# A hybrid RG-LRU, HGRN2 and SSD trunk: running decay sums spread to all partitions by DMA from a scratch in memory, in place of selector matmuls, with the other changes of the same edit

## The chip, the cores and the metric

One core of one Trainium2 chip runs the whole kernel. The metric is the device time of one execution in microseconds (us); each run is timed and the median of the runs is given. A profiled execution of the same program gives the trace.

## The reference, cut to what matters

The input is one sequence of 2048 tokens of width 1024; there is one layer. It normalises, applies shift and scale from a conditioning vector, projects to 5648 columns, runs three recurrent branches, concatenates them, projects back, adds through a gate, and normalises again.

```python
mod = cond @ w_ada[l] + b_ada[l]
shift, scale, gate = jnp.split(mod, 3, axis=-1)
h = rmsnorm(x, norm_w[l]) * (1.0 + scale[:, None]) + shift[:, None]
u = h @ w_in[l]
...
ya = rg_lru(xa, ...) * jax.nn.silu(a_g)              # LRU branch
yb = rmsnorm(hgrn2_chunked(q_h, k_in, hg_i, log_f)) * jax.nn.silu(hg_g)
yc = ssd_chunked(xs_h, dt, A, Bm, Cm)                # SSD branch
y = jnp.concatenate([ya, yb, yc], axis=-1) @ w_out[l]
x = x + gate[:, None] * y
```

The change is in the SSD branch. Per chunk of 128 tokens and per head it needs the running sum `cum` of the decays, once down the partitions and once along the columns:

```python
cum = jnp.cumsum(ai, axis=1)
diff = cum[:, :, None] - cum[:, None, :]
L = jnp.where(causal, jnp.exp(jnp.where(causal, diff, 0.0)), 0.0)
cb = jnp.einsum('btgn,bsgn->btsg', ci, bi)
y = jnp.einsum('btsg,btsgj,bsgjp->btgjp', cb, L, xi)
y = y + jnp.einsum('btgn,bgjpn,btgj->btgjp', ci, state, jnp.exp(cum))
```

## The kernel before

Everything is fp32. Each operand of a projection is split into a high and a low half in a matmul format (`fp32r`), and three matmuls (`PASSES`) make one product. Time is cut into four blocks (`tb`) of 512 tokens, and the kernel works on two halves of two blocks each. Per half it goes through stages: HGRN2 (projections `ps_v`, `ps_f`, `ps_q`, `ps_g`), SSD (`ps_bc`, then eight blocks of 128 channels, each with `ps_x` and `ps_z`), LRU (four blocks, `ps_lx` and `ps_lg`). At the end the output projection (`po`) runs over all.

The order on TensorE (PE) is written by hand: `weave` takes the list of projection matmuls of the current step and puts the small matmuls of the branches (generators such as `ssd_a`, `ssd_b`, `lru`, `norm_gen`) between them, one step behind the projections that feed them. A number beside a branch (`l0` for the gate matmuls of `lru`) says how many places it takes, and so how far the next of its matmuls comes after the last. The orders on VectorE (DVE), ScalarE (ACT), GpSimd (POOL) and SyncE (SP, which issues most DMAs) come out of a scheduler. The first stage, in which weights and inputs still arrive, follows the table `PROG`: `Xn` loads the input of block n, `Dk` a piece of the conditioning weights, `Ak` and `Ck` the matmuls and columns of piece k, `w` and `W` fetch and split projection weights, `S` and `R` make the norm of a block, `Hnk` makes k-th tile `ht` (high by ACT, low by DVE) of block n, `Mnk` its nine projection matmuls, `K` constants, `U` warm-up matmuls.

Names that matter below. `ssd_cr` makes the running sums of all 16 heads as rows (`d_cr`). For each SSD block, time block and head, `ssd_a` broadcasts one row to all partitions with a matmul against a selector (`ps_bcr`, L741; 64 of them), DVE subtracts the column sum and takes the minimum with 0, per chunk (`s_m`, L745), ACT makes `exp` of the broadcast row (`s_ce`) and of the difference (`s_m`), DVE multiplies `s_m` by the masked scores, POOL multiplies `s_ce` by C. `ssd_b` makes the state from `ps_bx` and then `ps_y` from `s_m` and `s_ce`. Small tiles share one ring of 32 slots of 2 KB per partition.

Between the halves, the input of blocks 2 and 3 is loaded, normalised and made into `ht` for the second half during the last LRU blocks: `norm_stats` squares the input on ACT (`xr`), `norm_rows` spreads the inverse norm to all partitions (`ps_rb`), DVE scales (`xt`) and makes the low half (`ht`). LRU has the gate matmuls `ps_r` and `ps_i` (L826, L827), which wait for the convolution (`cacc`) on DVE. HGRN2 of the next half begins with `ps_v`, whose last 8 columns (`dtr`) DVE copies out (L379).

## Time and profile before

| what | value |
|---|---|
| three timed runs | 1720.01, 1720.40, 1721.47 us |
| median | 1720.4 us |
| profiled execution, its own time | 1718.6 us |
| its span, first to last instruction | 1716.8 us |
| PE matmul busy | 1669.7 us (97%) |
| PE weight loads busy | 1362.3 us (79%) |
| DVE, ACT, POOL busy | 1083.1 (63%), 669.7 (39%), 768.3 us (45%) |
| mean granted clock of TensorE | 0.991 |

Shares are of the span. PE's weight loads run beside its matmuls. A share is a mean over stages that differ, so it does not tell by itself which engine is waited for in a stage.

### The profile page before, as it was taken

To read this page: it belongs to the slowest core of one execution; us is meant where nothing else is said; L and a number is where in the kernel's file an instruction comes from. 1 tells how busy PE (TensorE), PEld (TensorE's weight loads), DVE (VectorE), ACT (ScalarE), POOL (GpSimd) and SP (SyncE) were. 2 spreads that over 40 slices of the span, in tenths; PEclk is the share of its full clock that TensorE was granted. 3 is DMA by queue.
4 is the path that set the end of the run, shared out by engine and by line. 5 is a ranking of instruction groups with operands and counts; after the bars stand their busy time and mean duration, and the time that the engine had idled before them with its cause. 6 is when DMAs were issued, how large, how long until landed. Compare 5 with 4: busy or idle time off the path is not lost.

```text
span 1716.8 us, 29450 instructions
## 1 busy us (share of the span) xinstructions
PE 1669.7 (97%) x11520; PEld 1362.3 (79%) x11520; DVE 1083.1 (63%) x2042; ACT 669.7 (39%) x1346; POOL 768.3 (45%) x630
## 2 busy tenths in 40 slices
...
DMA packets 168492, 133.72 MB, mean 78 GB/s; under 512 B 13600, under 2 KB 136992, under 8 KB 168352
## 3 DMA queue, kind: packets, MB, share of 16 engines
...
## 4 chain that ended last, share of the span: by engine, by line
PE 84%; ACT 4%; DVE 4%; DMA 3%; issue 3%; POOL 2%; SPq 0%; ACTq 0%; POOLq 0%; DVEq 0%
PE po L1126 19%; PE ps_z L338 10%; PE ps_x L338 10%; PE ps_v L344 5%; PE ps_f L338 5%; PE ps_g L338 5%; PE ps_bc L338 5%; PE ps_q L338 4%; PE ps_lx L338 3%; PE ps_lg L338 2%; PE ps_y L789 2%; PE ps_bx L765 2%; PE ps_y L794 1%; PE ps_sA L562 1%; DVE xt L72 1%
## 5 line engine op out<-in xcount | busy, mean ns | idle before, releaser
L1126 PE MATMUL po<-wo,yy 128*128 128x512 f32 x1512 | 353.7, 396 | 2.6 <-POOL yy L69 1.6
L1126 PEld LDWEIGHTS po<-wo,yy 128*128 128x128 f32 x1512 | 284.0, 188 | 71.8 <-POOL yy L69 2.4
L69 POOL TENSOR_TENSOR w<-raw,w 128x512 fp32r<-128x512 f32 x156 | 223.5, 1451 | 209.3 <-ACT w L141 191.0
L72 DVE SCALAR_TENSOR_TENSOR cacc<-craw,col,cacc 128x512 f32<-128x512 f32 x192 | 205.9, 1079 | 47.7 <-ACT cacc L66 38.3
L338 PE MATMUL ps_x<-ht,w 128*128 128x512 f32 x768 | 192.4, 398 | 0.0
L338 PE MATMUL ps_z<-ht,w 128*128 128x512 f32 x768 | 189.8, 399 | 0.0
L338 PEld LDWEIGHTS ps_z<-ht,w 128*128 128x128 f32 x768 | 142.0, 189 | 33.4 <-issue 2.1
L338 PEld LDWEIGHTS ps_x<-ht,w 128*128 128x128 f32 x768 | 142.9, 189 | 29.9
L72 DVE SCALAR_TENSOR_TENSOR o<-po,rstd,o 128x512 f32<-128x512 f32 x64 | 47.3, 750 | 121.6 <-PE po L1126 103.1
L69 POOL TENSOR_TENSOR yy<-yr,yy 128x512 fp32r<-128x512 f32 x61 | 79.7, 1325 | 80.5 <-ACT yy L66 68.8
L69 POOL TENSOR_TENSOR hg_k<-hg_k,hg_t 128x256 f32<-128x256 f32 x80 | 59.1, 754 | 121.8 <-PE ps_sA L562 62.2
L338 PE MATMUL ps_f<-ht,w 128*128 128x512 f32 x384 | 99.6, 406 | 7.5 <-DVE ht L72 4.9
L344 PE MATMUL ps_v<-vw,ht 128*128 128x264 f32 x768 | 99.6, 290 | 4.8 <-DVE dtr L379 4.8
L141 ACT ACTIVATE w<-raw 128x512 fp32r<-128x512 f32 x156 | 90.3, 625 | 34.9 <-issue 22.3
L338 PE MATMUL ps_bc<-ht,w 128*128 128x512 f32 x384 | 101.2, 405 | 0.0
L344 PEld LDWEIGHTS ps_v<-vw,ht 128*128 128x128 f32 x768 | 96.3, 192 | 6.2 <-DVE dtr L379 5.0
L69 POOL TENSOR_TENSOR s_ce<-s_ce,cacc 128x512 f32<-128x512 f32 x64 | 100.1, 1581 | 1.1 <-ACT s_ce L66 0.8
L338 PE MATMUL ps_lx<-ht,w 128*128 128x512 f32 x384 | 99.5, 412 | 0.0
L338 PE MATMUL ps_q<-ht,w 128*128 128x512 f32 x384 | 99.2, 404 | 0.0
L338 PE MATMUL ps_lg<-ht,w 128*128 128x512 f32 x384 | 93.2, 398 | 0.0
L338 PE MATMUL ps_g<-ht,w 128*128 128x512 f32 x336 | 91.9, 408 | 0.0
L338 PEld LDWEIGHTS ps_f<-ht,w 128*128 128x128 f32 x384 | 70.9, 191 | 26.3 <-DVE ht L72 5.6
...
## 6 DMA issues: line engine op xcount, KB each, us to landing
raw<-in_w_in SPq DMA_DIRECT2D x176, 256.0 KB, 3.1
yr<-yscr SPq DMA_DIRECT2D x64, 256.0 KB, 3.2
xr<-in_x SPq DMA_DIRECT2D x48, 256.0 KB, 3.4
xt<-in_x_t SPq DMA_DIRECT2D x32, 256.0 KB, 5.3
wta<-in_w_mod SPq DMA_DIRECT2D x32, 256.0 KB, 5.3
yscr<-cacc ACTq DMA_DIRECT2D x32, 256.0 KB, 2.3
rawo<-in_w_out SPq DMA_DIRECT2D x32, 256.0 KB, 4.0
out<-o POOLq DMA_DIRECT2D x30, 256.0 KB, 3.6
```

The source lines that it names most:

```text
L69: e.tensor_tensor(o, a, b, op=op)
L72: V.scalar_tensor_tensor(o, a, s, b, op0=op0, op1=op1)
L141: after(V.tensor_copy(hi, raw) if eng is V else S.activation(hi, raw, AF.Copy), dep)
L338: d_ = PE.matmul(ps, b.hl[wl][:, k, :], ht[:, hl, :], start=(k == 0 and n == 0), stop=(k == KT - 1 and n == 2))
L344: d_ = PE.matmul(ps[:, 0:264], ht[:, hl, c * P:(c + 1) * P], b.vw[k // 4][wl][:, k % 4, :], start=(k == 0 and n == 0), stop=(k == KT - 1 a ...
L562: PE.matmul(out(n, c, r), Ks[n][:, o:o + 32], mv[n][..., o + sh:o + sh + 32], start=True, stop=True)
L765: PE.matmul(pkv[:, c].rearrange("p h n -> p (h n)"), bt[:, c], xw[:, c].rearrange("p h n -> p (h n)"), start=True, stop=True)
L789: PE.matmul(py[64 * hh:64 * hh + 64, c], xdt[:, c, hh], Ms[hh][:, c], start=True, stop=sv[tb][c] is None)
L794: PE.matmul(py[64 * hh:64 * hh + 64, c], sv[tb][c][:, 64 * hh:64 * hh + 64], Cs[hh][:, c * P:(c + 1) * P], start=False, stop=True)
L1126: PE.matmul(pss[t, n], yys[u, t][yl][:, k4, :], wts[4 * fam + k4][wl][n], start=(k4 == 0 and i == 0), stop=(k4 == 3 and i == 2))
```

## The change

The selector `sel`, its input `onehot_in` and the matmuls `ps_bcr` go. ACT copies the 16 rows of running sums to SBUF, a DMA writes them to a scratch in memory (`crd`), and for each SSD block, time block and head a DMA reads one row back with all 128 partitions as its destination (`s_cb`, 64 transfers of 256 KB). They are issued after the block's projections have been written down, ahead of the step in which `ssd_a` uses them. DVE's 256 subtractions become 256 `Relu` activations of 128x128 on ACT (scale -1, the column sum as bias), and the `exp` behind them takes scale -1.

Beside that: `PROG` is rewritten (weights of the second kind fetched later, `D2`, `X1` and the norm of block 0 earlier, constants `K` later), the softplus constants are made at the start (`early`) instead of in `consts`; `dtr` is copied by ACT instead of DVE; `norm_stats` of the second half moves from LRU steps 0 and 1 to SSD group 1, steps 1 and 2, and its inverse root to `norm_gen`; the second pair of gate matmuls of LRU step 2 in the first half comes later (`l0 = 2`), into another PSUM bank; two warm-up matmuls fewer; `split` on DVE makes the high half on ACT; `aneg` is made later.

```diff
-        cr = tmp("d_cr", (P, TB), F32R)
-        prf = pr.rearrange("p c n -> p (c n)")
-        V.tensor_copy(cr, prf)
-        for o in (32, 96):
-            tt(V, cr[o:o + 8], prf[o:o + 8], cr[o:o + 8], SUB)
-        return cr
+        cr = tmp("d_cr")
+        act(cr[0:16], pr.rearrange("p c n -> p (c n)")[0:16], AF.Copy)
+        nc.sync.dma_start(crd[tb], cr[0:16])
+
+    def ssd_cb(i, tb):
+        r = []
+        for hh in range(2):
+            cb = tmp("s_cb")
+            h_ = 2 * i + hh
+            nc.sync.dma_start(cb, crd[tb][h_:h_ + 1, :].to_broadcast([P, TB]))
+            r.append(cb)
+        return r
...
         for hh in range(2):
-            pb = bank(ps_sc, "sc", "ps_bcr", (P, 4, P))
-            PE.matmul(pb.rearrange("p c n -> p (c n)"), sel[:, g, 2 * j + hh:2 * j + hh + 1].to_broadcast([P, P]), cr,
-                      start=True, stop=True)
-            m = tmp("s_m", (P, 4, P))
+            m = cbs[tb][hh].rearrange("p (c n) -> p c n", n=P)
+            ce = tmp("s_ce")
+            act(ce, cbs[tb][hh], AF.Exp)
             for c in range(4):
-                V.tensor_scalar(m[:, c], pb[:, c], cum[:, c, h0 + hh:h0 + hh + 1], 0.0, op0=SUB, op1=MIN)
-            ce = tmp("s_ce")
-            act(ce, pb.rearrange("p c n -> p (c n)"), AF.Exp)
-            act(m, m, AF.Exp)
+                act(m[:, c], m[:, c], AF.Relu, scale=-1.0, bias=cum[:, c, h0 + hh:h0 + hh + 1])
+            act(m, m, AF.Exp, scale=-1.0)
             tt(V, m, m, gm, MUL)
             tt(G, ce, ce, C2, MUL)
...
-        V.tensor_copy(dtr[:, c, 8 * p:8 * p + 8], ps[:, 256:264])
+        act(dtr[:, c, 8 * p:8 * p + 8], ps[:, 256:264], AF.Copy)
...
+                if half == 0 and g == 1 and j in (1, 2):
+                    xst[j - 1] = norm_stats(1 + j)
...
                 sr = {}
-                pend = [(ssd_a(g, j, tb, xz[0, tb], bcg, dts[tb][0], sr), 2) for tb in tbs]
+                cbs = {tb: ssd_cb(4 * g + j, tb) for tb in tbs}
+                pend = [(ssd_a(g, j, tb, xz[0, tb], bcg, dts[tb][0], cbs, sr), 2) for tb in tbs]
...
-            if i < 2 and half == 0:
-                xst[i] = norm_stats(2 + i)
...
-            l0 = 5 if i == 3 and half == 1 else L0
+            l0 = 5 if i == 3 and half == 1 else 2 if i == 2 and half == 0 else L0
...
-PROG = ("X0 D0 w0 D1 w1 D2 S0 U8 A0 U1 C0 U2 R0 W0 D3 A1 U1 C1 H00 D4 W1 A2 M00 C2 H01 D5 A3 M01 C3 H02 D6 A4 M02 C4 "
-        "H03 D7 A5 M03 C5 H04 X1 A6 M04 C6 H05 S1 A7 M05 C7 H06 K M06 H07 R1 B M07 H10 H11 M10 H12 M11 H13 M12 H14 M13 "
-        "H15 M14 H16 M15 H17 M16 M17")
+PROG = ("X0 D0 w0 D1 D2 S0 U8 A0 Q0 U1 C0 D3 R0 W0 A1 U1 C1 H00 D4 A2 M00 C2 H01 w1 W1 D5 A3 M01 C3 H02 D6 A4 M02 C4 H03 X1 "
+        "A5 M03 C5 H04 D7 A6 M04 C6 H05 S1 M05 H06 Q1 A7 R1 M06 C7 H10 H07 B K M10 H11 M11 H12 M07 H13 M12 H14 M13 "
+        "H15 M14 H16 M15 H17 E M16 M17")
```

The rows of the orders follow at three places; an `x` and a number at the end of a row count equal rows in a run.

First place: PE in the SSD stage of the first half, the matmuls from the end of one block's `ps_z` to its `ps_bx`. Before:

```order
L338 MATMUL ps_z<-ht,w 128x512 x15
L733 MATMUL ps_xtr<-ident,cacc 128x128 x4
L741 MATMUL ps_bcr<-d_cr,sel 128x512
L338 MATMUL ps_x<-ht,w 128x512 x9
L741 MATMUL ps_bcr<-d_cr,sel 128x512
L338 MATMUL ps_x<-ht,w 128x512 x6
L733 MATMUL ps_xtr<-ident,cacc 128x128 x4
L741 MATMUL ps_bcr<-d_cr,sel 128x512
L338 MATMUL ps_x<-ht,w 128x512 x6
L741 MATMUL ps_bcr<-d_cr,sel 128x512
L338 MATMUL ps_x<-ht,w 128x512 x12
```

In the change:

```order
L339 MATMUL ps_z<-ht,w 128x512 x15
L739 MATMUL ps_xtr<-ident,cacc 128x128 x4
L339 MATMUL ps_x<-ht,w 128x512 x15
L739 MATMUL ps_xtr<-ident,cacc 128x128 x4
L339 MATMUL ps_x<-ht,w 128x512 x18
L768 MATMUL ps_bx<-s_xw,s_btok 128x128 x4
L339 MATMUL ps_x<-ht,w 128x512 x15
```

The four `ps_bcr` of a block are gone; the projections on either side of each stand together now.

Second place, between the halves: PE around the two pairs of gate matmuls (`ps_r`, `ps_i`) of LRU step 2 (steps count from 0). Before:

```order
L826 MATMUL ps_r<-cacc,wab 128x512
L827 MATMUL ps_i<-cacc,wab 128x512
L338 MATMUL ps_lx<-ht,w 128x512 x3
L826 MATMUL ps_r<-cacc,wab 128x512
L827 MATMUL ps_i<-cacc,wab 128x512
L338 MATMUL ps_lx<-ht,w 128x512 x21
L338 MATMUL ps_lg<-ht,w 128x512 x24
L338 MATMUL ps_lx<-ht,w 128x512 x24
L338 MATMUL ps_lg<-ht,w 128x512 x24
```

In the change:

```order
L829 MATMUL ps_r<-cacc,wab 128x512
L830 MATMUL ps_i<-cacc,wab 128x512
L339 MATMUL ps_lx<-ht,w 128x512 x21
L829 MATMUL ps_r<-cacc,wab 128x512
L830 MATMUL ps_i<-cacc,wab 128x512
L339 MATMUL ps_lx<-ht,w 128x512 x3
L339 MATMUL ps_lg<-ht,w 128x512 x24
L339 MATMUL ps_lx<-ht,w 128x512 x24
L339 MATMUL ps_lg<-ht,w 128x512 x24
```

Of the two gate pairs, the second stands behind 21 `ps_lx` now, where 3 stood before. At the same place, a little later, DVE's rows around the scaling of the input of block 3 (`xt`). Before:

```order
L72 SCALAR_TENSOR_TENSOR cacc<-craw,col,cacc 128x512
L69 TENSOR_TENSOR l_gs<-l_gs,ps_lg 128x512
L72 SCALAR_TENSOR_TENSOR cacc<-craw,col,cacc 128x512 x2
L72 SCALAR_TENSOR_TENSOR xt<-xt,gsc,rb 128x512 x8
L72 SCALAR_TENSOR_TENSOR ht<-xt,gsc,ht 128x512
L379 COPY dtr<-ps_v 128x8
L72 SCALAR_TENSOR_TENSOR ht<-xt,gsc,ht 128x512 x4
L379 COPY dtr<-ps_v 128x8
```

In the change:

```order
L72 SCALAR_TENSOR_TENSOR cacc<-craw,col,cacc 128x512
L69 TENSOR_TENSOR l_gs<-l_gs,ps_lg 128x512
L72 SCALAR_TENSOR_TENSOR cacc<-craw,col,cacc 128x512 x2
L285 RECIPROCAL xst<-xst 128x4
L72 SCALAR_TENSOR_TENSOR xt<-xt,gsc,rb 128x512 x8
L72 SCALAR_TENSOR_TENSOR ht<-xt,gsc,ht 128x512 x8
```

The copies of `dtr` have left DVE, and the reciprocal of the norm (`xst`), for which the second `ps_rb` waits, has come in behind the convolutions (`cacc`).

Third place, the start: DVE from the first scaling of block 1's input (`xt`) on. Before:

```order
L72 SCALAR_TENSOR_TENSOR xt<-xt,gsc,rb 128x512
L69 TENSOR_TENSOR sp_p<-sp_p,sp_w 128x4
L72 SCALAR_TENSOR_TENSOR xt<-xt,gsc,rb 128x512 x7
L136 TENSOR_SCALAR sp_p<-sp_p 128x4
L72 SCALAR_TENSOR_TENSOR hg_q<-hg_q,omlb,ps_q 128x512
L533 TENSOR_SCALAR hg_f<-hg_f,omlb 128x512
L72 SCALAR_TENSOR_TENSOR ht<-xt,gsc,ht 128x512
L72 SCALAR_TENSOR_TENSOR hg_g<-hg_g,col,ps_g 128x512
L72 SCALAR_TENSOR_TENSOR ht<-xt,gsc,ht 128x512 x2
```

In the change:

```order
L314 RECIPROCAL xsc<-xsc 128x4
L470 COPY maskd<-mf 128x32
L471 CAST masks<-mf 128x160
L72 SCALAR_TENSOR_TENSOR xt<-xt,gsc,rb 128x512 x7
L72 SCALAR_TENSOR_TENSOR ht<-xt,gsc,ht 128x512
L72 SCALAR_TENSOR_TENSOR gsc<-psm,col 128x1
L69 TENSOR_TENSOR gsc<-psm,col 128x1
L1048 TENSOR_SCALAR aneg<-aneg 128x16
L69 TENSOR_TENSOR gsc<-gsc,col 128x1
L72 SCALAR_TENSOR_TENSOR xt<-xt,gsc,rb 128x512 x2
L72 SCALAR_TENSOR_TENSOR ht<-xt,gsc,ht 128x512 x8
```

In both orders seven `xt` stand ahead of the first low half `ht` that follows; in the change the softplus rows (`sp_p`) are gone from between them, and the sign change of `aneg` (L1048) has come in.

## Rows read from the trace of the kernel before

**Rows 1.** The page's first part: busy time, share of span and instructions by engine.

```profile
PE 1669.7 (97%) x11520; PEld 1362.3 (79%) x11520; DVE 1083.1 (63%) x2042; ACT 669.7 (39%) x1346; POOL 768.3 (45%) x630
```

**Rows 2.** Windows: length; busy PE, PEld, DVE, ACT, POOL; clock; DMA share; GB/s.

```profile
0.00:50.00 50.00, 44.50 (x260) 26.22 (x261) 28.09 (x75) 23.96 (x45) 7.17 (x13) 1.00 0.93 311
50.00:100.00 50.00, 40.73 (x394) 34.67 (x393) 35.92 (x85) 19.29 (x39) 15.75 (x13) 0.90 0.31 82
350.00:450.00 100.00, 100.00 (x611) 83.30 (x610) 83.12 (x164) 44.72 (x93) 62.62 (x45) 1.00 0.19 53
650.00:750.00 100.00, 87.28 (x436) 71.65 (x435) 66.62 (x89) 57.08 (x105) 47.05 (x36) 0.91 0.28 77
```

**Rows 3.** Waits of PE: what it waited for, total us, times, longest us.

```profile
PE ps_f L338 <- DVE ht L72: 4.9, 2, 4.6
...
PE ps_f L338 <- ACT ht L330: 2.4, 2, 1.5
...
PE ps_rb L320 <- DVE sp_w L129: 2.0, 1, 2.0
```

**Rows 4.** Timeline of PE, one SSD block: start us, duration us, engine, line, operation.

```profile
400.35 0.48 PE L741 MATMUL ps_bcr<-d_cr,sel 128*128 128x512 f32 x1
400.67 2.26 PE L338 MATMUL ps_x<-ht,w 128*128 128x512 f32 x9
402.77 0.39 PE L741 MATMUL ps_bcr<-d_cr,sel 128*128 128x512 f32 x1
403.00 1.55 PE L338 MATMUL ps_x<-ht,w 128*128 128x512 f32 x6
```

**Rows 5.** The same timeline, later: the first ps_y of that block.

```profile
423.22 0.66 PE L789 MATMUL ps_y<-s_m,s_xdt 128*64 128x128 f32 x8
```

**Rows 6.** Timeline of DVE: the last product of scores and decay of that block.

```profile
410.58 1.12 DVE L69 TENSOR_TENSOR s_m<-s_m,s_gm 128x512 f32<-128x512 f32 x1 [0.34 <-ACT s_m L66]
```

**Rows 7.** Groups of ACT by form: xcount, then busy us and mean ns of one.

```profile
L66 ACT ACTIVATE hg_v<-ps_v 128x128 f32<-128x128 f32 x64 | 14.2, 273 | 70.2 <-PE ps_v L344 62.9 <-POOL l_gs L69 7.3
```

**Rows 8.** DMA issues: count, KB each, median us from issue to landing.

```profile
br<-in_rows SPq DMA_DIRECT2D x2, 256.0 KB, 4.2
```

**Rows 9.** Timeline of PE at the start; brackets: idle before, releaser.

```profile
54.78 1.63 PE L338 MATMUL ps_f<-ht,w 128*128 128x512 f32 x3
...
64.61 1.22 PE L338 MATMUL ps_f<-ht,w 128*128 128x512 f32 x2 [4.64 <-DVE ht L72]
65.63 1.48 PE L338 MATMUL ps_q<-ht,w 128*128 128x512 f32 x3
66.91 1.48 PE L338 MATMUL ps_g<-ht,wt 128*128 128x512 f32 x3
```

**Rows 10.** Timeline of DVE at the start: the scaling of block 1's input.

```profile
56.53 4.72 DVE L72 SCALAR_TENSOR_TENSOR xt<-xt,gsc,rb 128x512 f32<-128x512 f32 x7
```

**Rows 11.** Timeline of PE between the halves.

```profile
670.06 2.07 PE L826 MATMUL ps_r<-cacc,wab 128*128 128x512 f32 x2 [7.74 <-DVE cacc L72]
...
672.85 6.88 PE L338 MATMUL ps_lx<-ht,w 128*128 128x512 f32 x21
679.57 5.77 PE L338 MATMUL ps_lg<-ht,w 128*128 128x512 f32 x24
...
698.79 1.05 PE L320 MATMUL ps_rb<-ident,xst 128*128 128x128 f32 x8
699.60 8.27 PE L344 MATMUL ps_v<-vw,ht 128*128 128x264 f32 x66
712.65 5.07 PE L344 MATMUL ps_v<-vw,ht 128*128 128x264 f32 x24 [4.78 <-DVE dtr L379]
```

**Rows 12.** Timeline of DVE between the halves.

```profile
660.93 7.41 DVE L72 SCALAR_TENSOR_TENSOR xt<-xt,gsc,rb 128x512 f32<-128x512 f32 x8
...
699.72 2.68 DVE L72 SCALAR_TENSOR_TENSOR cacc<-craw,col,cacc 128x512 f32<-128x512 f32 x2
702.33 9.53 DVE L72 SCALAR_TENSOR_TENSOR xt<-xt,gsc,rb 128x512 f32<-128x512 f32 x8
```

More of the change, by code (lines that the diff above doesn't have):

```diff
@@ L88, in trunk @@
     rowp = cpool.tile([P, 32], F32, name="rowp")
-    ohf = cpool.tile([P, 2, 8], F32, name="ohf")
     wab = cpool.tile([P, 2, 4, P], F32, name="wab")
@@ L102, in trunk @@
     rstd = cpool.tile([P, 3, 16], F32, name="rstd")
+    crd = [dpool.tile([16, TB], F32, name=f"crd{i}") for i in range(NTB)]
     yscr = [dpool.tile([4, P, 16, P], F32, name=f"yscr{i}") for i in range(NTB)]
@@ L321, in norm_rows @@
         rb = tmp("rb")
-        d_ = S.activation(rb, ps, AF.Copy)
-        return rb, d_.ins.name
+        act(rb, ps, AF.Copy)
+        return rb
     def h_pre(xs, rb, k):
```

93 lines of the change are left out of this document (48 added, 45 removed).

## The prediction

> **What bounds the kernel now.** I read the page's busy times first. PE's matmuls take 97% of the span and no other engine more than 63% [rows 1], so time is won in two ways only: PE gets less to do, or it stands still less. The windows tell where each counts. In the SSD stage (350 to 450 us) PE is busy 100.00 of 100 us at the full clock, with DVE at 83.12 and ACT at 44.72 [rows 2]: there every matmul taken away is time taken away, as long as nothing else comes late. In two other windows PE has holes: 50 to 100 us (40.73 of 50 busy, granted clock 0.90) and 650 to 750 us (87.28 of 100, clock 0.91) [rows 2]. The list of PE's waits and the timelines name them. At the start PE waits for `ht`, by DVE 4.9 and by ACT 2.4 us, and 2.0 us for a softplus row ahead of the row of norms [rows 3]; 4.64 of the 4.9 is one wait [rows 9]. Between the halves it waits 7.74 us for `cacc` and 4.78 us for `dtr`, both on DVE [rows 11], and both times DVE is scaling eight `xt` tiles, 7.41 and 9.53 us [rows 12]. After such a hole PE runs at half clock (1.2 GHz) for a while: three matmuls start 1.28 us apart (65.63 to 66.91) [rows 9], where in the SSD stage nine take 2.10 us, that is 0.70 for three [rows 4].
>
> So there are three places, and the change touches each.
>
> **SSD stage.** 64 `ps_bcr` go, four in each of 16 blocks. What one costs is read from start to start in the timeline, since durations overlap: 0.32 us (400.35 to 400.67) and 0.23 us (402.77 to 403.00) [rows 4]; the other two of the block are alike (0.31 and 0.23). The mean of 0.27 gives 64 x 0.27 = **17.3 us**. Bounds: all at 0.23 give 14.7 us, and at the row's full 0.48 at most 31; as PE is without a hole there I take 17.3 and hold 14.7 to 20 for likely. The Trainium skill (TensorE: Matmul & The Clock Gate, Back-to-back issue gap) has a sustained spacing of some 131 ns for 512 columns; by that the 64 would be worth an estimated 8.4 us and the sum below 8.9 us less. The row speaks against it for this kernel: nine such matmuls in 2.10 us are 0.233 each [rows 4].
>
> The gain holds if the new way is hidden. DVE loses 256 subtractions, which only relieves it. ACT gets 16 `Relu` of 128x128 in each block. The nearest row is a copy of that shape, 64 in 14.2 us busy, 0.22 us each, 273 ns if alone [rows 7]: 3.6 to 4.4 us more on some 13.2 us of ACT in the 29.5 us of a block (44.72% [rows 2]), so 17 to 18, or 60%. The Trainium skill speaks against this move (ScalarE: Activation LUTs, Rules for kernel authors: simple arithmetic such as relu belongs on VectorE), and gives some 93 ns more for each operand that is a column. With that an estimated 5 us would be added to a block, which still leaves ACT idle for a third of it, so here the rule costs nothing by itself. The broadcasts, 64 of 256 KB, go to SP's queue among the weights. The nearest row is `br`, a row spread over all partitions in the same way: 4.2 us from issue to landing [rows 8]. They are issued about a step before they are needed. A block's last product of scores and decay ends at 411.70 (410.58 + 1.12) [rows 6], and the first `ps_y` that needs it starts at 423.22 [rows 5]: 11.5 us of slack before, and of the same order after. I cost them at nothing; if that cover is gone, the price is in the third rival.
>
> **Start.** The holes for `ht`, rb and ACT sum to 4.9 + 2.4 + 2.0 = 9.3 us [rows 3]. From 54.78 to the end of the three at 66.91 [rows 9] 18 matmuls run at half clock, at 1.28 - 0.70 = 0.58 us for each three: 3.5 us. So 12.8 us can be had. `D2` and the norm go ahead of the second weights `w1`, three transfers of 256 KB; at the 311 GB/s of the first 50 us [rows 2] these are 2.5 us, and I take 2 for the earlier start of the first projections. What stays: in the new order seven `xt` still stand ahead of the first low half of block 1, as the rows of the third place show, and they take 4.72 us [rows 10]. Input `X1` is moved past `D7`, four transfers of 256 KB, 3.4 us at that rate, so a part of the 4.72 is hidden: I keep 3.5 us of it. For `aneg`, which now stands among these rows and waits for the late load of `rowp`, I choose 1.2 us, with no row to size it, and 2.3 us for half clock after the hole: 7 in all. The start gains 12.8 + 2 - 7 = **7.8 us**, between 4 and 15.
>
> **Between the halves.** The second pair of gate matmuls stands 18 `ps_lx` later, 18 x 0.233 = 4.2 us more for DVE, and only five of the eight `xt` stand ahead of its `cacc`. The squares `xr` have left ACT at this place, so that the LRU chain runs ahead. I take the wait of 7.74 us as gone, and with it the half clock behind it: 21 `ps_lx` in 6.72 us (672.85 to 679.57) where 24 `ps_lg` take 5.77 at full clock, that is 5.05 for 21, so 1.7; the four gate matmuls take 2.79 (670.06 to 672.85), about twice their time, so 1.4 [rows 11]. With ACT copying `dtr`, the 4.78 us go too, and the half clock after them: 24 `ps_v` in 5.07 us against 66 in 8.27, or 3.0 for 24, so 2.1 us [rows 11]. Together 7.74 + 3.1 + 4.78 + 2.1 = 17.7 us.
>
> What is late next: the second `ps_rb` now needs the reciprocal of the norm, and that stands on DVE behind the two `cacc` that ended at 702.40 (699.72 + 2.68) [rows 12], while `ps_rb` itself started at 698.79 [rows 11]. With the same distance PE waits 3.6 us plus the reciprocal, 3.8 in all, and I add 2 us of half clock as after the hole for `dtr`. Left: 17.7 - 5.8 = **11.9 us**, between 6 (a second hole of this kind) and 17.7 (none).
>
> **Sum.** 17.3 + 7.8 + 11.9 = 37.0 us. The trace's own time is 1718.6 us (span 1716.8 and 1.8 around it), so 1681.6; the median of the runs shown lies 1.8 above the traced execution, so about **1683 us**.
>
> **The rivals.**
> *No hole is left.* Both `ps_rb` and the tiles of block 1 come in time: 17.3 + 14.8 + 17.7 = 49.8, which gives about 1671 us. For it: every wait named above has its cause moved. Against: the orders show `xt` ahead of `ht` and the reciprocal behind `cacc`.
> *The holes only move.* Projections are there in time but wait for another tile of the same engines: SSD at its lower bound 14.7, start 4, middle 2. That gives 20.7, about 1700 us. For it: DVE has the same eight `xt` and `ht` to do between the halves, busy 66.62 of 100 us [rows 2] with holes in PE all the same.
> *The broadcast chain becomes the bound of SSD.* ACT works in order. If a broadcast lands late, because SP's queue stands behind a slot of the ring that is not free, the `Relu` and `exp` that wait for it hold up ACT's evacuation of `ps_x`, and PE waits in each of 16 blocks. From 37.0 / 16 = 2.3 us a block on, the kernel is slower than before; at 3 us a block it is 1683 + 48 = 1731 us. For it: four slots of 32 are held a step longer, and ACT has more in its queue. Against: 11.5 us of slack [rows 5, 6] and ACT at 60%.
>
> **How the numbers follow.** Forecast 0.58, no hole 0.15, holes move 0.17, chain 0.10. A change under 0.2% (3.4 us) can't be told from none here. Of the chain's chance I give 0.06 to slower, 0.02 to the same and 0.02 to faster; the others are faster but for 0.01 of the moved holes: faster 0.91, same 0.03, slower 0.06. The range goes from 1668, just past the case without holes (SSD at 20 instead of 17.3), to 1703, just past the case of moved holes: it leaves out most of the chain and the tails of the others, some 0.15 to 0.2.
>
> **What would show it.** In the SSD windows PE stays at 100 of 100 us with no wait of `ps_y` or `ps_x` for `s_cb`, a block starts every 28.4 to 28.5 us in place of 29.54, and ACT's share is near 60. At the start `ps_f` still waits some 3 to 4 us for DVE's `ht`, and the first `ps_sA` comes some 7 us earlier. Between the halves no wait for `dtr` is left, the wait for `cacc` at `ps_r` is under 1 us, and `ps_rb` waits 3 to 5 us for the reciprocal. The prediction is wrong if `ps_y` waits for DVE or ACT in many blocks, or if a wait of over 5 us stands where none is named here.

## The result and the profile after

| | median | lowest to highest | runs |
|---|---|---|---|
| before | 1720.93 us | 1720.01 to 1721.68 | 4 |
| changed | 1700.57 us | 1699.24 to 1702.20 | 4 |

The changed kernel takes 0.9887 of the time before (95% interval 0.9875 to 0.9899): 20.4 us less. The forecast was 1683 us, 37 us less, in a range of 1668 to 1703. So the sign and the range held, the range by 2 us at its slow end, and little more than half (55%) of the gain that was added up came. The profiled execution has a span of 1697.5 us, 19.3 less than before.

The page's head, to be held against [rows 1]: busy time of each engine.

```profile
span 1697.5 us, 29336 instructions
...
PE 1653.0 (97%) x11452; PEld 1349.2 (79%) x11452; DVE 971.5 (57%) x1726; ACT 748.6 (44%) x1640; POOL 757.3 (45%) x630
```

PE has 16.7 us less to do, DVE 112 us less and ACT 79 us more. The windows, to be held against [rows 2]:

```profile
0.00:50.00 50.00, 41.13 (x230) 23.91 (x230) 28.78 (x94) 24.61 (x46) 6.11 (x12) 0.96 0.98 318
50.00:100.00 50.00, 41.62 (x338) 34.84 (x339) 33.13 (x57) 19.83 (x42) 15.70 (x12) 0.87 0.29 75
350.00:450.00 100.00, 100.00 (x611) 83.33 (x610) 65.31 (x120) 64.25 (x158) 61.90 (x47) 1.00 0.31 89
650.00:750.00 100.00, 94.49 (x479) 78.83 (x479) 60.91 (x82) 58.27 (x109) 46.53 (x37) 0.97 0.32 90
```

The SSD window is full as before, with DVE at 65.31 and ACT at 64.25. Between the halves PE is busy 94.49 us where it was 87.28. But the start, 0 to 100 us, is worse: 82.75 us busy in place of 85.23, at a lower clock. The list of PE's waits says why, to be held against [rows 3]:

```profile
PE ps_rb L320 <- DVE xst L285: 7.3, 2, 5.5
PE ps_f L339 <- DVE ht L72: 5.4, 1, 5.4
PE ps_ss L311 <- DVE xsq L305: 3.9, 1, 3.9
PE psm L450 <- ACT macc L66: 2.9, 1, 2.9
...
PE ps_z L339 <- ACT halo L66: 0.8, 1, 0.8
...
PE ps_y L792 <- DVE s_cb L69: 0.8, 1, 0.8
PE ps_xtr L739 <- DVE sst L72: 0.6, 1, 0.6
```

The waits for `cacc` (7.74 us) and `dtr` (4.78 us) [rows 11] are gone, and at the start those for ACT's `ht` (2.4) and the softplus row (2.0) [rows 3]. New are 7.3 us at `ps_rb`, 3.9 us for the squares of block 1 (`xsq`), 2.9 us for a column sum (`macc`), and 2.2 us in the SSD stage (`ps_z`, `ps_y`, `ps_xtr`). The wait for `ht` is still there.

Where the time went, by the starts of the same matmuls in the two traces (us; each line is a stretch up to the matmul named):

| up to | before | changed | this stretch | forecast |
|---|---|---|---|---|
| first `ps_sA` (start stage done) | 82.95 | 85.89 | +2.9 | -7.8 |
| first `ps_x` (HGRN2, half 1) | 314.54 | 317.56 | +0.1 | 0 |
| first `ps_r` (SSD, half 1) | 605.61 | 602.96 | -5.7 | -8.7 |
| `ps_f` of half 2 (between the halves) | 717.56 | 707.21 | -7.7 | -11.9 |
| first `po` (half 2, with its SSD) | 1344.3 | 1326.2 | -7.8 | -8.6 |
| end of span | 1716.8 | 1697.5 | -1.2 | 0 |

The lines that answer to [rows 4]: PE in one SSD block, with the start of `ps_bx` in this block and the next.

```profile
381.14 1.05 PE L768 MATMUL ps_bx<-s_xw,s_btok 128*128 128x128 f32 x8
...
401.22 0.60 PE L739 MATMUL ps_xtr<-ident,cacc 128*128 128x128 f32 x4
401.57 3.73 PE L339 MATMUL ps_x<-ht,w 128*128 128x512 f32 x15
405.14 0.60 PE L739 MATMUL ps_xtr<-ident,cacc 128*128 128x128 f32 x4
...
409.75 1.05 PE L768 MATMUL ps_bx<-s_xw,s_btok 128*128 128x128 f32 x8
```

A block takes 409.75 - 381.14 = 28.61 us, where it took 29.54 (the first `ps_y` of two blocks stood at 393.68 and 423.22, the second of them in [rows 5]). That is 0.93 less for four `ps_bcr`, 0.23 each and not 0.27. Why not 0.27 shows in the 15 `ps_x` behind the transposes: 405.14 - 401.57 = 3.57 us, 0.07 more than 15 x 0.233. In both kernels the matmul that stands first behind `ps_xtr` takes some 0.08 us more; before it was `ps_bcr` (0.32), now it is `ps_x`.

The start, to be held against [rows 9]: PE's waits and the first `ps_sA`.

```profile
23.19 0.96 PE L339 MATMUL ps_f<-ht,w 128*128 128x512 f32 x3
...
32.09 0.79 PE L450 MATMUL psm<-ones,macc 128*128 128x1 f32 x4 [2.94 <-ACT macc L66]
...
64.79 1.22 PE L339 MATMUL ps_f<-ht,w 128*128 128x512 f32 x2 [5.38 <-DVE ht L72]
...
85.89 0.65 PE L565 MATMUL ps_sA<-hg_q,hg_k 128*32 128x64 f32 x32
```

And ACT ahead of the first of them:

```profile
27.09 0.72 ACT L330 ACTIVATE ht<-xt,gsc 128x512 fp32r<-128x512 f32 x1 [3.39 <-DVE xt L72]
29.41 0.63 ACT L141 ACTIVATE w<-raw 128x512 fp32r<-128x512 f32 x1 [1.60 <-DMA raw<-in_w_in]
30.30 0.63 ACT L141 ACTIVATE w<-raw 128x512 fp32r<-128x512 f32 x1 [0.26 <-DMA raw<-in_w_in]
31.13 0.63 ACT L141 ACTIVATE wt<-raw 128x512 fp32r<-128x512 f32 x1 [0.21 <-DMA raw<-in_w_in]
31.67 0.37 ACT L66 ACTIVATE macc<-psm 128x256 f32<-128x256 f32 x1
```

The first projections start at 23.19, 2.7 us earlier than before, as forecast. But then ACT stands 1.60, 0.26 and 0.21 us for the second weights (`raw`), which the new table fetches later, splits them, and only then makes `macc` (31.67), for which PE has waited 2.94 us. Half clock follows: the three `ps_f` behind it take 1.46 us (34.67), where the first three took 0.96.

Between the halves, to be held against [rows 11, 12]: PE, then the reciprocal on DVE and the root on ACT ahead of it.

```profile
647.65 1.16 PE L320 MATMUL ps_rb<-ident,xst 128*128 128x128 f32 x8 [1.79 <-DVE xst L285]
...
665.73 1.02 PE L829 MATMUL ps_r<-cacc,wab 128*128 128x512 f32 x2
...
686.21 1.29 PE L345 MATMUL ps_v<-vw,ht 128*128 128x264 f32 x6
693.01 2.08 PE L320 MATMUL ps_rb<-ident,xst 128*128 128x128 f32 x8 [5.51 <-DVE xst L285]
...
707.21 5.02 PE L339 MATMUL ps_f<-ht,w 128*128 128x512 f32 x21
```

```profile
690.24 2.63 DVE L72 SCALAR_TENSOR_TENSOR cacc<-craw,col,cacc 128x512 f32<-128x512 f32 x2
692.79 0.17 DVE L285 RECIPROCAL xst<-xst 128x4 f32<-128x4 f32 x1
```

```profile
689.72 0.69 ACT L152 ACTIVATE l_r<-ps_r,col 128x512 f32<-128x512 f32 x1 [2.08 <-POOL l_gs L69]
...
692.29 0.30 ACT L152 ACTIVATE xst<-xst,epsc 128x4 f32<-128x4 f32 x1
```

The second gate pair (665.73) waits no more. The second `ps_rb` waits 5.51 us, from 687.50 on, and runs at half clock (2.08 us, where the first took 1.16): its reciprocal came at 692.79, right behind the root on ACT (692.29 + 0.30), which stands behind gate activations and a table load, and behind the two `cacc`, which end at 692.87 (690.24 + 2.63; neighbouring rows overlap a little). So the two `cacc` alone would have held it about as long.

### The profile page after: what moved, and what is told of

It reads as the page before. It is cut to its first block, busy times and chain, and to the rows that moved or that the text cites. A ratio compares the mean times of both kernels' runs of the same rounds, so it can differ in the third digit from the quotient of the medians.

```text
span 1697.5 us, 29336 instructions
## 1 busy us (share of the span) xinstructions
PE 1653.0 (97%) x11452; PEld 1349.2 (79%) x11452; DVE 971.5 (57%) x1726; ACT 748.6 (44%) x1640; POOL 757.3 (45%) x630
## 4 chain that ended last, share of the span: by engine, by line
PE 85%; DVE 4%; DMA 3%; ACT 3%; issue 3%; POOL 2%; SPq 0%; POOLq 0%; ACTq 0%; DVEq 0%
PE po L1138 19%; PE ps_x L339 10%; PE ps_z L339 9%; PE ps_v L345 6%; PE ps_f L339 5%; PE ps_g L339 5%; PE ps_bc L339 5%; PE ps_q L339 4%; PE ps_lg L339 4%; PE ps_lx L339 4%; PE ps_y L792 2%; PE ps_bx L768 2%; PE ps_y L797 1%; PE ps_sA L565 1%; PE ps_o L645 1%
## 5 line engine op out<-in xcount | busy, mean ns | idle before, releaser
L1138 PEld LDWEIGHTS po<-wo,yy 128*128 128x128 f32 x1512 | 283.8, 188 | 71.5 <-POOL yy L69 2.4
L142 POOL TENSOR_TENSOR w<-raw,w 128x512 fp32r<-128x512 f32 x156 | 219.6, 1426 | 266.9 <-ACT w L141 223.4
L339 PEld LDWEIGHTS ps_x<-ht,w 128*128 128x128 f32 x768 | 141.1, 189 | 28.6
L69 POOL TENSOR_TENSOR s_ce<-s_ce,cacc 128x512 f32<-128x512 f32 x64 | 93.5, 1481 | 1.5 <-ACT s_ce L66 1.5
```

Of the source, the lines that this page charges most:

```text
L69: e.tensor_tensor(o, a, b, op=op)
L142: after(eng.tensor_tensor(lo, raw, hi, op=SUB), dep if eng is V else None)
L339: d_ = PE.matmul(ps, b.hl[wl][:, k, :], ht[:, hl, :], start=(k == 0 and n == 0), stop=(k == KT - 1 and n == 2))
L1138: PE.matmul(pss[t, n], yys[u, t][yl][:, k4, :], wts[4 * fam + k4][wl][n], start=(k4 == 0 and i == 0), stop=(k4 == 3 and i == 2))
```

## The experiments

All times are medians; a ratio is to the kernel before, timed beside each run (1719.6 to 1720.8 us), with its 95% interval. "By the spans" compares the two profiled executions.

**e1, the named change alone** on the kernel before: rows by broadcast in place of `ps_bcr`, and the exponent on ACT.

```diff
-            PE.matmul(pb.rearrange("p c n -> p (c n)"), sel[...].to_broadcast([P, P]), cr,
-                      start=True, stop=True)
...
+            nc.sync.dma_start(cb, crd[tb][h_:h_ + 1, :].to_broadcast([P, TB]))
+                act(m[:, c], m[:, c], AF.Relu, scale=-1.0, bias=cum[:, c, h0 + hh:h0 + hh + 1])
+            act(m, m, AF.Exp, scale=-1.0)
```

> The kernel before with the named change alone: rows by DMA from the scratch, Relu on ACT, no selector matmuls; start table, dtr on DVE, norm statistics and gate places as before. Theory 1 (each removed matmul is worth its bare pitch of 0.23 us and nothing comes late): 64 x 0.23 = 14.7 us, and the 1.1 us of waits for ps_bcr go too, so 1720.9 - 15.8 = 1705 us; a block of the SSD stage starts every 28.6 us. Rival 1 (0.27 us each, as the forecast took): 1720.9 - 18.4 = 1702.5 us and 28.45 us a block. Rival 2 (the broadcast chain makes waits in SSD that eat part of it): over 1709 us, with waits of ps_y or ps_x for s_cb or for ACT in several blocks.

Measured: 1703.28 us, ratio 0.9905 (0.9888 to 0.9923), 17.5 us less by the medians and 14.7 by the spans (1716.8 to 1702.1). Its blocks:

```profile
378.21 1.05 PE L766 MATMUL ps_bx<-s_xw,s_btok 128*128 128x128 f32 x8
...
406.81 1.05 PE L766 MATMUL ps_bx<-s_xw,s_btok 128*128 128x128 f32 x8
```

28.60 us a block: theory 1, 0.23 us for each matmul. The median lies nearer to rival 1's 1702.5 than to theory 1's 1705, but the blocks are not rival 1's 28.45, and the spans give 14.7. In SSD only two waits of `ps_y`, 1.3 us in all, are for the new way, so rival 2 falls.

**e2, each selector matmul twice** on the kernel before.

```diff
-            PE.matmul(pb.rearrange("p c n -> p (c n)"), sel[...].to_broadcast([P, P]), cr,
-                      start=True, stop=True)
+            for _ in range(2):
+                PE.matmul(pb.rearrange("p c n -> p (c n)"), sel[...].to_broadcast([P, P]),
+                          cr, start=True, stop=True)
```

> The kernel before with each of the 64 selector matmuls issued twice into the same bank (the work is only repeated). It prices one matmul by itself, without the new way. Theory 1 (0.23 us each): 1720.9 + 14.7 = 1735.6 us. Rival 1 (0.27 each): 1738.2 us. Rival 3 (the Trainium skill, TensorE: Matmul & The Clock Gate, Back-to-back issue gap: 131 ns for 512 columns): an estimated 1729.3 us. A second one behind the same weights could also cost less than the first; then it lies under 1735.

Measured: 1736.81 us, ratio 1.0093 (1.0078 to 1.0108), 16.1 us more (spans: 16.1 too), and 30.48 us a block:

```profile
353.36 1.05 PE L766 MATMUL ps_bx<-s_xw,s_btok 128*128 128x128 f32 x8
...
383.84 1.05 PE L766 MATMUL ps_bx<-s_xw,s_btok 128*128 128x128 f32 x8
```

That is 0.94 more for four, 0.24 each; over all, 16.1 / 64 = 0.25. The 16.1 us lie between theory 1 and rival 1, but 2.0 of them come ahead of the first SSD block (first `ps_x` at 316.58 us against 314.54), where nothing was repeated; the blocks speak for theory 1. The 0.131 of the Trainium skill (TensorE: Matmul & The Clock Gate, Back-to-back issue gap), by an estimate 8.4 us, are not what this kernel pays.

**e3, the start table of before** on the changed kernel, with `Q0` and `Q1` put ahead of `R0` and `R1`. `Q` is the sums over partitions (`ps_ss`) with their root, in the new table a step of its own; the table of before also lacks `E`, which puts the first sigmoids on ACT behind the last `ht`. The first line of each table:

```diff
-PROG = ("X0 D0 w0 D1 D2 S0 U8 A0 Q0 U1 C0 D3 R0 W0 A1 U1 C1 H00 D4 A2 M00 C2 H01 w1 W1 D5 A3 M01 C3 H02 D6 A4 M02 C4 H03 X1 "
...
+PROG = ("X0 D0 w0 D1 w1 D2 S0 U8 A0 U1 C0 U2 Q0 R0 W0 D3 A1 U1 C1 H00 D4 W1 A2 M00 C2 H01 D5 A3 M01 C3 H02 D6 A4 M02 C4 "
...
```

> The changed kernel with the start table PROG of before (the norm's two halves stand together, as before); all else as changed. Theory 1 (the table's later fetch of the second weights makes ACT wait in order with their split, so that the columns macc come late, and the squares of block 1 behind them): the waits of 2.9 us for macc and 3.9 us for xsq go, the first projections start 2.7 us later again, and the start is that of before or a little better: 1700.6 - 3 = 1697.6 us, at best 1695. Rival (the loss in the start comes from the constants made early or from the high halves on ACT, not from the table): 1700.6 us, with waits of the same size at the start.

Measured: 1700.28 us, ratio 0.9874 (0.9855 to 0.9893), its runs from 1695.93 to 1701.7. By time it can't be told from the changed kernel, which is the rival's time and not theory 1's 1697.6. By its trace the start ends at 83.95 us, 1.9 earlier than in the changed kernel, and the wait for `xsq` is gone, but `macc` still costs 3.3 us in three waits, against theory 1, and `ht` 6.2; and 2.6 us more go in the output projection, which the table does not touch. The end of the start differs between traces too: the six with the start of the change (changed, e4, e8, e10, e11, e12) have it at 84.1 to 88.3 us, the three with the old one (before, e1, e2) at 83.0 to 83.4. So e3 leaves open what the table costs; e6 and e7 show a part of it.

**e4, both inverse roots early** on the changed kernel.

```diff
+            if i == 1 and half == 0:
+                xst = {n_: rsqrt_cols(xst[n_]) for n_ in xst}
...
-        rb = norm_rows(rsqrt_cols(st))
+        rb = norm_rows(st)
```

> The changed kernel with the inverse roots of the norms of blocks 2 and 3 made in LRU step 1 of the first half, not right ahead of the matmuls ps_rb; all else as changed. Theory 1 (PE waits 1.8 and 5.5 us at ps_rb only because the reciprocal stands on DVE behind convolutions, and ACT's root behind gate activations): both waits go, and some 1.1 us of half clock, so 1700.6 - 8.4 = 1692.2 us. Rival (the holes only move: DVE and ACT have the same work there, so ps_v, ps_f or ps_r wait instead): 1698 to 1700.6 us, with a new wait of over 4 us between 640 and 730 us.

Measured: 1693.40 us, ratio 0.9842 (0.9827 to 0.9856), 7.2 us less than the changed kernel. No wait at `ps_rb` is left and none of over 0.7 us comes in its place between 640 and 730 us; from the first `ps_r` to the `ps_f` of half 2 it takes 95.2 us, where the changed kernel takes 104.3. Theory 1.

**e5, `xt` tile by tile** on e4.

```diff
-    def h_pre(xs, rb, k):
-        stt(xs[k], xs[k], gsc[:, 1, k:k + 1], rb, MUL, MUL)
+    def h_pre(xs, rb, k, dep=None):
+        after(V.scalar_tensor_tensor(xs[k], xs[k], gsc[:, 1, k:k + 1], rb, op0=MUL, op1=MUL), dep)
...
+                        h_pre(xsb[ar[0]], sts[ar[0]], ar[1], lo[-2] if ar[0] == 1 and ar[1] > 1 else None)
```

> The changed kernel with the early inverse roots of the run before (1693.4 us) and one thing more: at the start the k-th scaling of block 1's input on DVE stands behind the low half of tile k-2, so that two xt stand ahead of the first ht, not seven. Theory 1 (PE waits 5.0 to 5.4 us for ht because seven xt stand ahead of it, and runs at half clock after it): the wait falls under 1.5 us and about 2 us of half clock go: 1693.4 - 6 = 1687.4 us. Rival (each tile now goes DVE, ACT, DVE, over 2.1 us a tile, so PE, which takes 2.1 us a tile, waits a little at each of seven): 1690 to 1693 us, with many short waits of ps_f for ht.

Measured: 1693.95 us, ratio 0.9852 (0.9837 to 0.9867): no difference from e4. The wait of 5 us splits in two, which is neither of the two things expected:

```profile
64.02 0.50 PE L341 MATMUL ps_f<-ht,w 128*128 128x512 f32 x1 [2.18 <-ACT ht L330]
66.53 1.22 PE L341 MATMUL ps_f<-ht,w 128*128 128x512 f32 x2 [2.01 <-DVE ht L332]
```

The first is for ACT's high half. ACT's row has the split of the `v` weights and the constants ahead of that tile, so the seven `xt` were not all that made the tiles late. My reading of this wait, in the prediction too, named half of it.

**e6, the split of the second weights a tile later** on e5.

```diff
-PROG = ("X0 D0 w0 D1 D2 S0 U8 A0 Q0 U1 C0 D3 R0 W0 A1 U1 C1 H00 D4 A2 M00 C2 H01 w1 W1 D5 A3 M01 C3 H02 D6 A4 M02 C4 H03 X1 "
+PROG = ("X0 D0 w0 D1 D2 S0 U8 A0 Q0 U1 C0 D3 R0 W0 A1 U1 C1 H00 D4 A2 M00 C2 H01 w1 D5 A3 M01 C3 H02 W1 D6 A4 M02 C4 H03 X1 "
```

> As the kernel of the run beside it, and the split of the second weights (W1) written one tile later in the start table, so that ACT makes the columns macc of pieces 2 and 3 ahead of it; the fetch stays where the change put it. Theory 1 (ACT waits in order for weights that the change fetches later, and with it macc, PE's next matmuls, and through the later tiles the squares of block 1): the waits of 2.9 us (macc) and 3.9 us (xsq) shrink to under 2 us together, some 1.5 us of half clock go: 4 to 6 us less than the run beside it, so some 1682 us. Rival (the inputs are late anyway, so that the holes only move to another wait before 55 us): within 1.5 us of the run beside it.

Measured: 1687.42 us, ratio 0.9813 (0.9797 to 0.9829), 6.5 us less than e5. No wait for `macc` is left, so theory 1 holds on the cause; the wait for `xsq` (3.9 us) stands unchanged, so that it does not hang on the first one, as theory 1 had it. The start ends at 79.27 us, against 85.37 in e5.

**e7, the second weights fetched early** on e5.

```diff
-PROG = ("X0 D0 w0 D1 D2 S0 U8 A0 Q0 U1 C0 D3 R0 W0 A1 U1 C1 H00 D4 A2 M00 C2 H01 w1 W1 D5 A3 M01 C3 H02 D6 A4 M02 C4 H03 X1 "
+PROG = ("X0 D0 w0 D1 w1 D2 S0 U8 A0 Q0 U1 C0 D3 R0 W0 A1 U1 C1 H00 D4 A2 M00 C2 H01 W1 D5 A3 M01 C3 H02 D6 A4 M02 C4 H03 X1 "
```

> As e5, with the second weights fetched early again (between D1 and D2, as before the change) and split at the place that the change gives. The first projections start some 2.5 us later, as there are 0.75 MB more ahead of them. Theory 1 (the later fetch is what ACT waits for): the waits for macc and xsq go, against 2.5 us of later start: 2 to 3 us less than e5, some 1685 us. Rival (the fetch is not the cause): e5 plus 2.5 us, some 1690.

Measured: 1689.48 us, ratio 0.9827 (0.9811 to 0.9843), 4.5 us less than e5, with no wait for `macc` and the first projections at 25.4 us. The two intervals just overlap, but the start ends at 81.36 us, 4.0 earlier than in e5. Theory 1 by another way, but for `xsq`, whose wait stays at 3.9 us: the later fetch, split at its place, costs more than the earlier start gives.

**e8, the squares back in the LRU** on the changed kernel, with the roots behind them; it differs from e4 by the place of the squares.

```diff
-                if half == 0 and g == 1 and j in (1, 2):
-                    xst[j - 1] = norm_stats(1 + j)
...
+            if i < 2 and half == 0:
+                xst[i] = rsqrt_cols(norm_stats(2 + i))
```

> The changed kernel with the squares of blocks 2 and 3 back in LRU steps 0 and 1 of the first half, with their inverse roots right behind them; all else as changed, the later second pair of gate matmuls too. It differs from e4 (1693.4 us) by the place of the squares. Theory 1 (the squares on ACT hold up the gate activations of the LRU, and with them cacc for the second pair): a part of the wait for cacc comes back, 7.7 - 4.2 = 3.5 us, and the 2 us of waits in the SSD stage that the squares bring there go: 1693.4 + 1.5 = 1695 us. Rival (the later pair alone removes the wait; the move of the squares gives nothing): 1693.4 - 2 = 1691.4 us with no wait for cacc of over 1 us.

Measured: 1698.07 us, ratio 0.9876 (0.9859 to 0.9893), 4.7 us more than e4. The wait for `cacc` comes back:

```profile
668.23 2.04 PE L829 MATMUL ps_r<-cacc,wab 128*128 128x512 f32 x2 [4.39 <-DVE cacc L72]
```

and of SSD's waits 0.5 us is left. By the starts of the same matmuls e8 takes 7.3 us more than e4 from the first `ps_r` to the `ps_f` of half 2, and 2.8 us less from the first `ps_x` to the first `ps_r`. So of the 7.74 us the moved squares take away 4.4, and the rest, 3.3, falls to the later gate pair (4.1 if held against the 8.5 of e1), by difference, as no run moves that pair alone; the squares cost 2 to 3 us in SSD. Theory 1; its 1695 us left out the half clock behind the wait, here 2.04 us for two matmuls that take 1.02 without it.

**e9, constants and `v` weights a few tiles later** on e6.

```diff
-         "A5 M03 C5 H04 D7 A6 M04 C6 H05 S1 M05 H06 Q1 A7 R1 M06 C7 H10 H07 B K M10 H11 M11 H12 M07 H13 M12 H14 M13 "
+         "A5 M03 C5 H04 D7 A6 M04 C6 H05 S1 M05 H06 Q1 A7 R1 M06 C7 H10 H07 M10 H11 M11 H12 M07 H13 B K M12 H14 M13 "
```

> As e6 (1687.4 us), with the constants K and the load of the v weights B written after the tile H13, not ahead of M10, in the start table, so that ACT's split of these weights no longer stands ahead of the tiles 1 to 3 of block 1. Theory 1 (ACT's in-order row holds the tiles: in e5 and e6 PE waits 2.2 us for ACT's ht and 2.0 us for DVE's behind it): both waits fall under 1 us together, 1 to 2 us of half clock go: 1687.4 - 4.5 = 1683 us. Rival (the v weights and aneg now come late for ps_v and the first decays, with two more table loads on ACT): 1687 us or more, with a new wait at ps_sA or ps_v between 80 and 95 us. The wait of 3.9 us for xsq stays by both.

Measured: 1684.28 us, ratio 0.9792 (0.9777 to 0.9806), 3.1 us less than e6: the fastest of all, 36 us under the kernel before. Its interval just overlaps that of e6; the waits decide. The start now:

```profile
47.11 1.84 PE L311 MATMUL ps_ss<-ones,xsq 128*128 128x1 f32 x8 [3.83 <-DVE xsq L305]
...
58.32 0.50 PE L341 MATMUL ps_f<-ht,w 128*128 128x512 f32 x1 [0.28 <-ACT ht L330]
59.82 0.74 PE L341 MATMUL ps_f<-ht,w 128*128 128x512 f32 x2 [1.00 <-DVE ht L332]
...
76.48 0.65 PE L567 MATMUL ps_sA<-hg_q,hg_k 128*32 128x64 f32 x32
```

The two waits for `ht` take 1.28 us together, and the start ends at 76.48 us, 2.8 earlier than in e6 and 6.5 earlier than before, not far from the 7.8 that the forecast had given to the change.

**e10, the subtractions back on DVE**, rows still by DMA.

```diff
-                act(m[:, c], m[:, c], AF.Relu, scale=-1.0, bias=cum[:, c, h0 + hh:h0 + hh + 1])
-            act(m, m, AF.Exp, scale=-1.0)
+                V.tensor_scalar(m[:, c], m[:, c], cum[:, c, h0 + hh:h0 + hh + 1], 0.0, op0=SUB, op1=MIN)
+            act(m, m, AF.Exp)
```

> The changed kernel with the 256 subtractions back on DVE (minus the column sum, minimum with 0, from the broadcast tile in SBUF) and exp with scale 1 on ACT; rows still by DMA. Theory 1 (PE is the bound in SSD and neither engine is waited for, so the place of the exponent's arithmetic is worth nothing but the 2 us of waits that ACT's load makes beside the squares): 1699 to 1700.6 us, 28.6 us a block. Rival 4 (ACT's load is what gives or costs time in SSD): more than 4 us away from 1700.6, with waits of PE for DVE or none for ACT.

Measured: 1717.76 us, ratio 0.9989 (0.9979 to 0.9998). All but 2.4 us of the gain is gone. Theory 1 falls. The signs of rival 4 came, a time far off and waits of PE for DVE, but what costs the time is DVE's load and not ACT's. From the first `ps_x` to the first `ps_r` the two halves take 294.3 and 294.7 us, where the changed kernel takes 285.4 and 283.8 and the kernel before 291.1 in both: with the subtraction on DVE, rows by DMA are slower in SSD than the selector matmuls were. The subtraction as a group, first in the kernel before (from PSUM), then here (from SBUF); busy and mean ns of one stand behind the bar:

```profile
L745 DVE TENSOR_SCALAR s_m<-ps_bcr,d_all 128x128 f32<-128x128 f32 x256 | 70.7, 340 | 3.5 <-PE ps_bcr L741 3.3 <-issue 0.3
```

```profile
L750 DVE TENSOR_SCALAR s_cb<-s_cb,d_all 128x128 f32<-128x128 f32 x256 | 155.5, 671 | 30.2 <-POOL acc L69 21.0 <-ACT s_ce L66 7.8 <-POOL w L142 0.7
```

One takes 671 ns on the mean instead of 340, and DVE stands idle ahead of them for 21.0 us that the profile puts down to POOL. One after another, with POOL beside it:

```profile
409.58 4.53 DVE L750 TENSOR_SCALAR s_cb<-s_cb,d_all 128x128 f32<-128x128 f32 x4 [3.13 <-POOL acc L69]
...
414.64 4.25 DVE L750 TENSOR_SCALAR s_cb<-s_cb,d_all 128x128 f32<-128x128 f32 x4
...
419.41 1.65 DVE L750 TENSOR_SCALAR s_cb<-s_cb,d_all 128x128 f32<-128x128 f32 x8
```

```profile
412.77 2.52 POOL L69 TENSOR_TENSOR s_ce<-s_ce,cacc 128x512 f32<-128x512 f32 x2
```

Four take 4.53 and 4.25 us while POOL works on tiles in SBUF, without a break from 409.26 to 418.81, and eight take 1.65 us right behind. PE then waits for DVE's state (`ps_y` for `s_st`, 14 times, 8.4 us), and 1.5 us at `ps_bx` for POOL's `s_xw`. The whole trace says the same: of the 256 subtractions, the 137 that no tile operation of POOL overlaps take 269 to 280 ns each, the 119 others 1128 on the mean, and 115 of these end some 0.08 us behind the end of a POOL operation. In the kernel before, where DVE read the same numbers from PSUM, POOL's operations overlap all 256, and each takes 332 to 354 ns. The Trainium skill (Perfetto Trace Analysis, Optimizing Scalar/DVE Operations) says that GpSimd and VectorE share a read port to SBUF; these numbers agree with it. No run takes POOL's work away.

**e11, each broadcast twice** on the changed kernel.

```diff
             nc.sync.dma_start(cb, crd[tb][h_:h_ + 1, :].to_broadcast([P, TB]))
+            nc.sync.dma_start(cb, crd[tb][h_:h_ + 1, :].to_broadcast([P, TB]))
```

> The changed kernel with each broadcast of a row issued twice into the same tile, the second behind the first (work is only repeated); so a row comes some 4 us later, and SP's queue stands still for as long at each. Theory 1 (some 11 us of slack at ps_y and SP's queue not full): 1700.6 to 1702 us, ps_y waits under 2 us more in all. Rival 2 (the broadcast chain is near its limit): over 1706 us, with waits of ps_y for s_cb in many blocks or of ps_x for weights.

Measured: 1702.42 us, ratio 0.9899 (0.9885 to 0.9914), 0.4 us over the range of theory 1 and far from rival 2, but not where it was expected: one wait of `ps_z` for ACT grows from 0.8 to 4.7 us, behind the moved squares, and no block waits at `ps_y`. The first half's SSD stage takes 2.9 us longer, the second's as long as in the changed kernel. Ahead of that wait ACT stands 4.19 and 3.65 us for the squares' inputs `xr`, which SP issues too; in the changed kernel it stands there 4.70 us once. The chain has slack, and the tightest place is there.

**e12, everything but the named change.**

```diff
-            m = cbs[tb][hh].rearrange("p (c n) -> p c n", n=P)
+            pb = bank(ps_sc, "sc", "ps_bcr", (P, 4, P))
+            PE.matmul(pb.rearrange("p c n -> p (c n)"), sel[...].to_broadcast([P, P]), cr,
+                      start=True, stop=True)
...
```

> The changed kernel with the named change undone: selector matmuls and the subtractions on DVE from PSUM as before, everything else of the change (start table, early constants, dtr on ACT, moved squares and roots, later gate pair) kept. Theory 1 (the two halves of the change lie in different stages and add up): the changed kernel gained 20 us, the named change alone 17, so the rest alone gives some 3 us: 1716 to 1718 us, with the waits of the changed kernel at the start (macc 2.9, xsq 3.9, ht 5.4) and at ps_rb (1.8 and 5.5). Rival (they help or hurt each other: the squares now share the SSD stage with four more subtractions a row on DVE): outside 1714 to 1719 us, with waits in the SSD stage that neither kernel has.

Measured: 1714.78 us, ratio 0.9971 (0.9959 to 0.9983): 5.3 us less than before, 1.2 us under what theory 1 gave. With e1's 17.5 that makes 22.8 where both together gave 20.4, so the two parts add up to within some 2 us, which these medians hardly tell from nothing; by the spans it is 4.4 + 14.7 = 19.1 against 19.3. Its waits in SSD are 3.3 us at `ps_bcr` for ACT, beside the squares, where before had 1.1.

## Why the forecast held and where its sum failed

The sum had three terms, 17.3 + 7.8 + 11.9 = 37.0 us. What each measured:

**SSD stage: mechanism right, 0.23 for 0.27.** The gain is the bare pitch, 64 x 0.233 = 14.9 us, the lower bound of the forecast (14.7), shown by the blocks of e1 and the changed kernel (28.6 us) and from the other side by e2. The waits that the squares brought into the first half's SSD stage (2.2 us with them, 0.5 without, e8) were not in the sum: I had called the move of the squares a gain for the LRU and put no price on the place where they went. The cover held: no block waits at `ps_y` even with the rows later (e11), and ACT is at 64% of the window against 60 forecast. A `Relu` took 392 ns, and 0.31 us each in a row, where I had taken 0.22 to 0.27 from a copy without a column as operand:

```profile
L66 ACT ACTIVATE s_cb<-s_cb,d_all 128x128 f32<-128x128 f32 x256 | 79.2, 392 | 0.4
```

The Trainium skill's estimate for one with such an operand (ScalarE: Activation LUTs, What ACT_TABLE_LOAD costs), 280 + 0.833 x 128 = 387 ns, agrees with that row. Its rule that relu belongs on VectorE (Rules for kernel authors) does not hold for this kernel: e10 follows it, and that costs 17 us. Where it meets no operation of POOL, a subtraction is faster on DVE (274 ns) than a `Relu` on ACT (392), as the rule has it; the meetings turn that round. That ACT takes the subtraction is the half of the change that makes the other one worth having, and of the rule I had written that here it "costs nothing by itself". I had no row of a DVE subtraction from SBUF beside POOL, and did not ask for the price of leaving it there.

**Start: the step that failed.** "What stays: in the new order seven `xt` still stand ahead of the first low half of block 1": I gave the change 7.8 us, and it lost 2.9 (by the spread in e3, between 1 and 5). I followed the order of PE and DVE and the fetches on SP's queue, but not the splits on ACT, which stand in its order ahead of `macc` and wait for the weights that the table fetches later. e6 and e7 show the price, 6.5 and 4.5 us. The 2 us for an earlier start of the projections came, as 2.7. Of the 18 matmuls that the sum took at half clock, three from 57.48 on take 1.14 us, where half clock would be 1.48, and the one at 59.47 takes 0.50, so that its 3.5 us are some 0.5 too much.

The wait for `ht` kept 5.38 us against 3.5 in the sum. The 4.72 us of the seven `xt` were taken from before; in the change they take 6.75:

```profile
57.32 6.75 DVE L72 SCALAR_TENSOR_TENSOR xt<-xt,gsc,rb 128x512 f32<-128x512 f32 x7 [3.56 <-ACT rb L66]
```

Two of them, 1.77 and 1.75 us where the others take 0.75, overlap POOL's low halves of the `v` weights (59.31 to 62.74), which fall there in the new order; before, POOL began with them at 60.38, when the `xt` were all but done. So of this wait some 2.0 us, by an estimate, is POOL's, and the 3.5 of the sum would have been about right without it. ACT's splits of the same weights hold up the tiles behind (e5, e9). The 1.2 us chosen for `aneg` came to nothing: it stands behind the first `ht`.

The wait for the squares of block 1 (3.9 us, `xsq`) was in no part of the forecast. The squares are hardly later: DVE's last sum ends at 50.46 us before and at 51.05 in the change. PE is there earlier, since the new table puts `Q1` ahead of the matmuls of piece 7 and of the nine projections of a tile (`M06`), which stood ahead of `ps_ss` before. Before, then in the change:

```profile
50.22 0.86 PE L338 MATMUL ps_g<-ht,wt 128*128 128x512 f32 x3
50.92 0.95 PE L311 MATMUL ps_ss<-ones,xsq 128*128 128x1 f32 x8
```

```profile
46.45 0.86 PE L339 MATMUL ps_g<-ht,wt 128*128 128x512 f32 x3
51.19 1.83 PE L311 MATMUL ps_ss<-ones,xsq 128*128 128x1 f32 x8 [3.88 <-DVE xsq L305]
...
56.41 0.94 PE L339 MATMUL ps_f<-ht,w 128*128 128x512 f32 x3
```

With the old place (e3) the wait is gone, with the new one (e6, e7, e9) it stays at 3.8 to 3.9 us; no run moves `Q1` alone.

**Between the halves: mechanism right, one wait too small and one not seen.** The wait for `cacc` went, by the two causes named (e8: 4.4 us by the squares, the rest by the gate pair), and that for `dtr` too. The new wait at the second `ps_rb` was forecast at 3.8 us and measured 5.51: the sum kept the distance of before, the two `cacc` ending 3.6 us behind PE's arrival, and in the change they end 5.4 behind it, with ACT's root, which the sum had not looked at, done only 0.3 us earlier. The first `ps_rb`, costed at nothing, waits 1.79. Both are waits without need, as e4 shows: 7.2 us.

**The rivals.** "The holes only move" gave 1700 us and the kernel took 1700.6, at 0.17 against 0.58 for the forecast, which held only because its range reached to this rival. That the rival's time is so near is luck in its turn: its SSD at the lower bound came, but it had the start at 4 us gained and the middle at 2, and the start lost 2.9 while the middle gained 7.7. Of the signs set down beside it, the waits that should go went; a block (28.61 us), the end of the start and the waits at `ht` and `ps_rb` came out worse than stated. The chain of broadcasts as the bound did not come (e11), and what "no hole is left" supposed (1671 us) is not reached by e9 either: 1684 us, with four edits more.
